# Loads and small stages of a decoder layer's input projection moved to other steps of its plan

## The chip, the cores and the metric

One core of a Trainium2 chip. The metric is the device time of one execution, in microseconds (us), as the median of several runs. The engines are TensorE (PE, with its weight loads PEld), VectorE (DVE), ScalarE (ACT), GpSimd (POOL) and SyncE (SP), which only issues DMAs. Each engine and each issuing queue takes its instructions in program order.

## The reference

One layer of a decoder on 2048 prompt rows and on 8 samples of 4 rows each, all in float32. What matters here is its beginning: an RMS norm, one input projection to five column groups, a layer norm and a gating product on one of them, and for the samples attention over a cache of 2048 keys.

```python
def _project(x, g, w_in):
    z = _rmsnorm(x, g) @ w_in
    return jnp.split(z, [D_ATT, 2 * D_ATT, 3 * D_ATT, 3 * D_ATT + D_SGU], axis=-1)
...
def _spatial_gate(vc, w_s, b_s):
    T = vc.shape[-3]
    causal = jnp.tril(jnp.ones((T, T), dtype=w_s.dtype))
    wm = w_s[:, :T, :T] * causal
    return jnp.einsum('gts,...sgc->...tgc', wm, vc) + b_s[:, :T].T[:, :, None]
...
    q, k, v, u, vg = _project(x, norm1_g, w_in)
    ...
    att = _merge_branches(outs, lses).reshape(B, S, D_ATT).astype(x.dtype)
    vn = _layernorm(vg, sgu_ln_g, sgu_ln_b)
    vn = vn.reshape(B, S // CHUNK, CHUNK, N_GROUPS_SGU, SGU_GROUP_DIM)
    gate = _spatial_gate(vn, sgu_w, sgu_b).reshape(B, S, D_SGU)
    x = x + jnp.concatenate([att, u * gate], axis=-1) @ w_out
    x = x + _swiglu(x, norm2_g, w_gate, w_up, w_down)
```

In the attention, scores get a bias by relative distance from a small table (`rel_bias`), masked where no key lies; for the samples the three dilated branches are taken in one softmax.

## The kernel before

The kernel runs three long parts one after another: the input projection, the prompt's attention, and the output projection with the feed-forward. The change is all in the first.

**The plan.** The first part is written as a plan of about 240 steps. `at(step, phase, fn)` puts a function into it; `Plan.run` sorts by step, then by phase (early, exp, low, scores, turn, mid, values, out, misc, store), then by the order of the `at` calls, and calls each. The scheduling is manual, so this is also each engine's program order. An instruction that waits holds up whatever follows it on its engine; a DMA whose buffer is not free holds up whatever follows it on its queue. Nearly all DMAs go out on SP; the sample's query loads (L530) and the four new rows of a key tile (L519) go out on ACT.

**The projection.** Two halves of 8 row tiles (128 rows each); in each half the five column groups, in the order q, k, u, g, v and then u, g, q, k, v; for each column group the row tiles in groups of 3, 3 and 2; for each of these 8 steps, one for each 128 rows of the weights (k). So a column group is 24 steps, a half is 120. A step's `products` (L318 to L320) are three matmuls for each row tile, since each operand is split into a high and a low part (xh*wh, xh*wl, xl*wh); in the first half the groups of two also take the samples' rows (L323), two matmuls. Results go to PSUM: two double banks (`ps_s`) in turn, and two single ones (`ps_o`) for the third of a group. A bank must be read out before the next group but one may write it.

**Weights.** Piece n (0 to 79) is 128 x 512, loaded by `w_load` (L215) and split into `wh` by ACT (L220) and `wl` by DVE (L226), six steps ahead of its first use. Pieces 0 to 7 are loaded at the very beginning into two wide tiles (`w_first`, four slots each). All others go through `raw` tiles, of which there are three, nine steps ahead of their use. The wide tiles serve again for the split gate rows (`vnh`, `vnl`) from step 84.

**What follows the products.** q and k are scaled by ACT (`zn`, L330), transposed on PE (L344), split (L349, L350) and stored. u is scaled (L402). g is scaled in PSUM (L334) and then goes through a layer norm: statistics on DVE (`layer_norm_a`, L366), a square root on ACT (L374), a product on DVE that frees the bank (`layer_norm_c`, L379), scale and bias on ACT and POOL (L382, L383). `gate_split` splits the result on ACT (`vnh`, L135) and POOL (`vnl`, L138). For each group of four row tiles follow four gate products on PE (`gates`, L412), their bias and product with u on DVE (`gates_u`, L420), four transposes (`gated`, L426), copies and stores. The small results on PE (`ps_t`) share two banks in turn.

**Tables and masks.** `gate_loads` (L263 to L271) and `gate_diagonal` (L274) fetch the gate's matrices, `gate_masks` masks and splits them. `table` (L482) makes the prompt's bias rows, stored by L485; `table_spread` (L488, L489) copies them from DRAM to DRAM into one shifted row per partition and head, 1024 rows of 640 and 1024 rows of 128 numbers. `sample_table` (L501) makes the samples' bias `bias_s`.

**The samples.** For each sample b and row t, `key_unit` (L536) multiplies a query with three key tiles (u = 0, 1, 2), and `key_sum` (L541) adds up over each head on DVE. The u = 0 units run on DVE, most others on POOL. For samples 0 to 2 the units u = 1, 2 run at steps 36 to 59 and u = 0 at 60 to 74; from sample 3 on, from step 76, all three run together, three units in four steps, to step 155. A key tile is loaded three steps ahead (L518, L522). Then come `sample_bias` (L557), the softmax for each half of the samples (`softmax_a`, `_e`, `_b`, `_c`: L562 to L584, with an exponential on ACT), and products with the values (L596).

The lines of the plan that are touched are the calls of `at` near L642 to L673, L723 to L729 and L759 to L766.

Of the kernel before, what the change touches and what calls it, by code (L numbers as in the profile page):

```python
# [10 lines left out]
F32 = mybir.dt.float32  # L11
# [8 lines left out]
P = 128  # L20
# [3 lines left out]
KD = D // P  # L24
H = 8
# [4 lines left out]
SB = 8  # L30
ST = 4
# [33 lines left out]
def hymba_step(ctx: ExitStack, tc: tile.TileContext, A: dict, O: dict):  # L65
# [9 lines left out]
    turn = [0, 0, 0, 0]  # L75
# [85 lines left out]
    at = plan.at  # L161
# [13 lines left out]
    def raw_tile():  # L175
        return rp.tile([P, 512], F32, name="raw", tag="raw", bufs=RAW)
# [32 lines left out]
    W = {}  # L209

    def w_load(n):
        half, ki, k = n // (5 * KD), n // KD % 5, n % KD
        c0 = COL[ORDER[half][ki]]
        W[n, "r"] = r = raw_tile()
        sync.dma_start(r, A["w_in"][k * P:(k + 1) * P, c0:c0 + 512])  # L215

    def w_high(n):
# [335 lines left out]
        unit["hm"] = sp.tile([P, DA], F32, name="hm", tag="kn", bufs=2)  # L553
        sync.dma_start(unit["hm"], A["headmask"])

    def sample_bias():
        dve.tensor_add(S, S, bias_s.broadcast_to([P, 3, SB, ST * H]))  # L557

    def softmax_a(bg):
        pt = ps_t()  # L560
# [80 lines left out]
                x_half(*first[n][1:])  # L641
    for n in range(KD, 2 * 5 * KD):  # L642
        need = n // KD * 24 + n % KD
        at(need - 9, "misc", w_load, n)
        at(need - 6, "early", w_high, n)
        at(need - 6, "mid", w_low, n)
    for t, s0, s1 in ((3, -1, 1), (4, 0, 2), (5, 2, 5), (6, 6, 10), (7, 8, 13)):
# [11 lines left out]
        at(s0, "early", norm1_scale, a, b)  # L659
    at(12, "misc", sample_load)  # L660
    at(15, "out", sample_split)
    at(42, "misc", gate_loads)
    for b in range(SB):
        at(44 + b, "misc", gate_diagonal, b)
    at(54, "out", gate_masks)
    at(56, "misc", table_loads)
    at(60, "turn", table, 0, 512, l12_d[:, 0:512])
    at(61, "turn", table, 512, 256, l12_d[:, 512:768])
    at(62, "turn", table, 768, 256, l3_d)
    at(63, "misc", sample_table_load)  # L670
    at(65, "misc", table_spread)
    at(70, "turn", sample_table)

    V0 = 168
    for s0, r in ((V0 - 1, [0]), (170, [0, 3]), (B0, [0, 1])):
# [2 lines left out]
    for half in range(2):  # L678
        for ki, kind in enumerate(ORDER[half]):
            for gi, tiles in enumerate(GROUPS):  # L680
# [13 lines left out]
                for j, tj in enumerate(tiles):  # L694
# [15 lines left out]
                    if kind in "qk":  # L710
                        which = "qk".index(kind)
                        at(e + 1, "turn", transposed, which, kind, t)
                        if kind == "k":
                            at(e + 1, "store", store_rows, kind, t)
                        at(e + 2, "early", transposed_split, which, t)
                        at(e + 2, "store", store_transposed, which, t)
                    elif kind == "v":
                        at(e + 1, "store", store_values, t)
                        at(e + 1, "store", store_rows, kind, t)
                    else:  # L720
                        layer_norm(e + 1, t, lambda t=t: zn["g", t], P, lambda t=t: gate_tile(t))

                        f = e + 4 + (3 if tj in (4, 5) else 0)  # L723
                        at(f, "turn", gate_split, t)
                        if tj % 4 == 3:
                            g = t // 4
                            for x in range(4):
                                at(f + 2 + x, "turn", gates, g, x)
                                at(f + 3 + x, "early", gates_u, g, x)  # L729
                            for x in range(4):  # L730
                                at(f + 6 + x, "turn", gated, g, x)
                                at(f + 7 + x, "early", gated_copy, g, x)
                                at(f + 7 + x, "store", store_gated, g, x)
# [13 lines left out]
    for run in key_runs:  # L747
        for j, (b, t, u) in enumerate(run):
# [7 lines left out]
            at(s0, "out", key_unit, b, t, u, pool if u == 1 or u == 2 and b >= EARLY else dve)  # L756
            at(s0 + 1, "out", key_sum, b, t, u)
            i += 1
    at(159, "early", sample_bias)  # L759
    at(159, "out", values_start)  # L760
    for bg in range(2):
        s0 = V0 - 8 + bg * 32
        at(s0, "turn", softmax_a, bg)
        at(s0 + 1, "early", softmax_e, bg)
        at(s0 + 3, "early", softmax_b, bg)
        at(s0 + 5, "turn", softmax_c, bg)  # L766
# [1314 lines left out]
```

## Time and profile before

| | |
|---|---|
| median of 3 runs | 2550.32 us (2549.67 to 2557.51) |
| profiled execution, its time | 2553.33 us |
| its span, first to last instruction | 2551.4 us |
| PE busy | 2447.2 us (96%) |
| DVE, ACT, POOL busy | 1275.1, 1129.6, 1292.2 us (50, 44, 51%) |
| mean granted TensorE clock | 0.984 |
| DMA moved | 455.37 MB, mean 178 GB/s |

How to read the profile. A row of the timeline is: start in us from the span's start, duration, engine, source line, operation, result and operands, shapes, count, and in brackets the idle time of the engine just before it with what ended it. SPq and ACTq are DMAs being issued on these queues; their duration is that of the issue, not of the transfer. A row of the windows is: the stretch, its length, the busy time of PE, weight loads, DVE, ACT and POOL with the number of instructions, the granted share of the TensorE clock, the busy share of the 16 DMA engines, and GB/s. Idle time of an engine that is not the bottleneck costs nothing by itself.

### The profile page before, as it was taken

To read this page: it belongs to the slowest core of one execution; us is meant where nothing else is said; L and a number is where in the kernel's file an instruction comes from. 1 tells how busy PE (TensorE), PEld (TensorE's weight loads), DVE (VectorE), ACT (ScalarE), POOL (GpSimd) and SP (SyncE) were. 2 spreads that over 40 slices of the span, in tenths; PEclk is the share of its full clock that TensorE was granted. 3 is DMA by queue.
4 is the path that set the end of the run, shared out by engine and by line. 5 is a ranking of instruction groups with operands and counts; after the bars stand their busy time and mean duration, and the time that the engine had idled before them with its cause. 6 is when DMAs were issued, how large, how long until landed. Compare 5 with 4: busy or idle time off the path is not lost.

```text
span 2551.4 us, 39141 instructions
## 1 busy us (share of the span) xinstructions
PE 2447.2 (96%) x14022; PEld 2120.1 (83%) x14022; DVE 1275.1 (50%) x2598; ACT 1129.6 (44%) x2438; POOL 1292.2 (51%) x1012
## 2 busy tenths in 40 slices
PE   8999999999999898999999999999999998999997
PEld 6777786667888678899899988999999986999996
DVE  4448674216777644443444465444444465444445
ACT  6414333226666556545445355332323345444432
POOL 2116442004777636667677543553645534666662
PEclk9999999999999899999999999999999998999998
DMA  8964735675554463536546471563544543665552
GB/s 260 281 220 150 255 115 164 200 252 197 174 178 151 116 205 112 182 128 198 169 143 201 139 220 62 203 214 128 204 163 160 203 152 122 224 206 192 197 193 106
DMA packets 292149, 455.37 MB, mean 178 GB/s; under 512 B 28695, under 2 KB 160968, under 8 KB 286836
## 3 DMA queue, kind: packets, MB, share of 16 engines
q1 hardware_dynamic: 285108, 440.82, 52.7%
q10 hardware_dynamic: 6848, 12.06, 1.6%
q8 instruction: 111, 1.82, 0.3%
q14 instruction: 82, 0.67, 0.1%
HBM read 365.07 MB, written 157.84 MB: 205 GB/s over the span
## 4 chain that ended last, share of the span: by engine, by line
PE 55%; POOL 9%; issue 7%; ACT 4%; DVE 4%; DMA 2%; SPq 0%; POOLq 0%; ACTq 0%; DVEq 0%
PE ps_o L1647 13%; PE ps_m L1576 8%; PE ps_m L1575 8%; PE ps_m L1574 8%; POOL op L1517 3%; PE ps_s L853 2%; PE ps_o L908 2%; DMA ab_d<-pair 2%; ACT fr L1485 1%; PE ps_t L880 1%; PE ps_s L932 1%; POOL pair L1497 1%; POOL pair L1506 1%; POOL fr L1500 1%; POOL dw L138 1%
## 5 line engine op out<-in xcount | busy, mean ns | idle before, releaser
L1517 POOL TENSOR_TENSOR op<-fr,op 128x512 fp32r<-128x512 f32 x385 | 488.3, 1297 | 313.2 <-ACT op L1513 291.6
L1574 PE MATMUL ps_m<-xh,op 128*128 128x384 f32 (+3 forms) x1904 | 605.2, 318 | 0.0
L1575 PE MATMUL ps_m<-xl,op 128*128 128x384 f32 (+3 forms) x1904 | 604.2, 317 | 0.9 <-POOL xl L138 0.9
L1576 PE MATMUL ps_m<-xh,op 128*128 128x384 f32 (+3 forms) x1904 | 604.6, 318 | 0.0
L1647 PE MATMUL ps_o<-dw,hw 128*128 128x512 f32 x2040 | 484.0, 392 | 15.7 <-DVE acc L1649 14.4
L1647 PEld LDWEIGHTS ps_o<-dw,hw 128*128 128x128 f32 x2040 | 379.5, 188 | 98.6 <-DVE acc L1649 20.7
L1575 PEld LDWEIGHTS ps_m<-xl,op 128*128 128x128 f32 x1904 | 360.3, 189 | 4.8 <-POOL xl L138 1.1
L1574 PEld LDWEIGHTS ps_m<-xh,op 128*128 128x128 f32 x1904 | 360.7, 189 | 4.0
L1576 PEld LDWEIGHTS ps_m<-xh,op 128*128 128x128 f32 x1904 | 360.1, 189 | 0.1
L1649 DVE TENSOR_TENSOR acc<-acc,ps_o 128x512 f32<-128x512 f32 (+1 forms) x362 | 247.1, 686 | 214.8 <-PE ps_o L1647 214.8
L1614 ACT ACTIVATE ps_t<-zn 128x384 f32<-128x384 f32 (+1 forms) x126 | 58.3, 463 | 462.1 <-DVE zn L1597 361.9
L1513 ACT ACTIVATE op<-fr 128x512 fp32r<-128x512 f32 x396 | 235.7, 623 | 24.4 <-DMA fr<-ab_d 19.7
L138 POOL TENSOR_TENSOR dw<-fd,dw 128x1024 fp32r<-128x1024 f32 x66 | 158.5, 2402 | 121.7 <-ACT dw L135 121.7
L318 PE MATMUL ps_s<-wh,xh 128*128 128x512 f32 x480 | 199.7, 416 | 10.6 <-ACT xh L135 6.0
L319 PE MATMUL ps_s<-wl,xh 128*128 128x512 f32 x480 | 191.7, 399 | 1.8 <-DVE wl L226 1.8
L320 PE MATMUL ps_s<-wh,xl 128*128 128x512 f32 x480 | 191.3, 399 | 0.0
L1517 POOL TENSOR_TENSOR op<-pair,op 128x512 fp32r<-128x512 f32 x63 | 81.4, 1301 | 116.4 <-ACT op L1513 116.4
L318 PEld LDWEIGHTS ps_s<-wh,xh 128*128 128x128 f32 x480 | 92.5, 193 | 54.2 <-issue 23.7
L536 POOL TENSOR_TENSOR pr<-kv,qb 96x512 f32<-96x512 f32 x32 | 47.2, 1479 | 178.1 <-DMA qb<-zs_d 61.6
L1624 ACT ACTIVATE hw<-ps_t 128x384 fp32r<-128x384 f32 (+1 forms) x126 | 56.1, 453 | 175.1 <-DVE ps_t L1620 174.1
L924 POOL CAST sq<-k 128x512 fp32r<-128x512 f32 x32 | 34.0, 1062 | 164.3 <-PE ps_s L319 164.3
L320 PEld LDWEIGHTS ps_s<-wh,xl 128*128 128x128 f32 x480 | 92.3, 192 | 20.6 <-DVE xl L138 0.3
(456 smaller groups left out, 4296.6 us busy)
## 6 DMA issues: line engine op xcount, KB each, us to landing
fr<-ab_d SPq DMA_DIRECT2D x308, 256.0 KB
fd<-in_w_down_dram SPq DMA_DIRECT2D x66, 512.0 KB
out_ks_dram<-in_cache_k_dram SPq DMA_DIRECT2D x56, 512.0 KB
out_vs_dram<-in_cache_v_dram SPq DMA_DIRECT2D x56, 512.0 KB
ab_d<-fr SPq DMA_DIRECT2D x88, 256.0 KB
raw<-in_w_in_dram SPq DMA_DIRECT2D x72, 256.0 KB
qk_d<-pair SPq DMA_DIRECT2D x64, 256.0 KB
ab_d<-pair SPq DMA_DIRECT2D x63, 256.0 KB
```

Of the source, the lines that this page charges most:

```text
L138: (eng_lo or pool).tensor_sub(lo, src, hi.bitcast(F32))
L318: pe.matmul(o[j], xh[:, k, :], wh, start=(k == 0), stop=False)
L319: pe.matmul(o[j], xh[:, k, :], wl, start=False, stop=False)
L320: pe.matmul(o[j], xl[:, k, :], wh, start=False, stop=(k == KD - 1))
L1513: act.activation(ops[f, j][0], ab[f][j], AF.Copy)
L1517: (pool if f or j in POOL_LOW else dve).tensor_sub(lo_, ab[f][j], hi.bitcast(F32))
L1574: pe.matmul(out, wh[:, ks], xh[:, :, k], start=(k == 0), stop=False)
L1575: pe.matmul(out, wh[:, ks], xl[:, :, k], start=False, stop=False)
L1576: pe.matmul(out, wl[:, ks], xh[:, :, k], start=False, stop=(k == 3))
L1614: act.activation(g, c, AF.Silu)
L1647: pe.matmul(ps[0:nr], l_, r_[:, cs], start=(z == 0 and y == 0), stop=(z == FC - 1 and y == len(pairs) - 1))
L1649: dve.tensor_add(B.acc[i][0:nr, cs], B.acc[i][0:nr, cs], ps[0:nr])
```

## The change

- Weight pieces 8 to 31 (the other column groups k, u, g of the first half) are loaded into the eight slots of the first wide tiles and not into `raw`, and earlier: pieces 8 to 15 at steps 6 to 20 (before: 15 to 22), 16 to 23 at steps 19 to 40 (39 to 46), 24 to 31 at steps 43 to 64 (63 to 70). The splits stay where they are.
- `gate_loads`, `gate_diagonal` and `gate_masks` go five steps later; `table_loads` from 56 to 62, `table` from 60-62 to 70-72, `sample_table_load` from 63 to 73, `table_spread` from 65 to 75, `sample_table` from 70 to 82.
- In the first half the gate products of both groups of four go two steps later (first group 94 to 96, second 104 to 106), with all that follows them; the split of tiles 4 and 5 goes two steps later too.
- `sample_bias` is done for each half of the samples, at steps 134 and 159 (before: once, at 159), and the first half's softmax runs at steps 136 to 141 (before 160 to 165). The second half's stays at 192.

```diff
-        W[n, "r"] = r = raw_tile()
+        W[n, "r"] = r = w_first[k // 4][:, k % 4].bitcast(F32) if n < 4 * KD else raw_tile()
...
-    def sample_bias():
-        dve.tensor_add(S, S, bias_s.broadcast_to([P, 3, SB, ST * H]))
+    def sample_bias(bg):
+        s = S[:, :, bg * 4:bg * 4 + 4]
+        dve.tensor_add(s, s, bias_s.broadcast_to([P, 3, 4, ST * H]))
...
-        at(need - 9, "misc", w_load, n)
+        at(max(need - 29 + 2 * (n % KD), 6 + 2 * (n % KD)) if n < 4 * KD else need - 9, "misc", w_load, n)
...
-    at(42, "misc", gate_loads)
+    at(47, "misc", gate_loads)
     for b in range(SB):
-        at(44 + b, "misc", gate_diagonal, b)
-    at(54, "out", gate_masks)
-    at(56, "misc", table_loads)
-    at(60, "turn", table, 0, 512, l12_d[:, 0:512])
-    at(61, "turn", table, 512, 256, l12_d[:, 512:768])
-    at(62, "turn", table, 768, 256, l3_d)
-    at(63, "misc", sample_table_load)
-    at(65, "misc", table_spread)
-    at(70, "turn", sample_table)
+        at(49 + b, "misc", gate_diagonal, b)
+    at(59, "out", gate_masks)
+    at(62, "misc", table_loads)
+    at(70, "turn", table, 0, 512, l12_d[:, 0:512])
+    at(71, "turn", table, 512, 256, l12_d[:, 512:768])
+    at(72, "turn", table, 768, 256, l3_d)
+    at(73, "misc", sample_table_load)
+    at(75, "misc", table_spread)
+    at(82, "turn", sample_table)
...
-                        f = e + 4 + (3 if tj in (4, 5) else 0)
+                        f = e + 4 + ((3 if half else 5) if tj in (4, 5) else 0)
                         at(f, "turn", gate_split, t)
                         if tj % 4 == 3:
                             g = t // 4
+                            f += (2, 2, 0, 0)[g]
                             for x in range(4):
                                 at(f + 2 + x, "turn", gates, g, x)
...
-    at(159, "early", sample_bias)
+    at(134, "early", sample_bias, 0)
+    at(159, "early", sample_bias, 1)
...
-        s0 = V0 - 8 + bg * 32
+        s0 = (136, V0 + 24)[bg]
```

## The prediction, made before the changed kernel was run

> **What bounds the kernel now.** I read the page first, then the TensorE rows that begin with idle time, then busy time by windows, then the queues around each wait. TensorE (PE) is busy 96% of the span, so the time is the work of PE plus what PE waits.
>
> ```profile
> PE 2447.2 (96%) x14022; PEld 2120.1 (83%) x14022; DVE 1275.1 (50%) x2598; ACT 1129.6 (44%) x2438; POOL 1292.2 (51%) x1012
> ...
> PEclk9999999999999899999999999999999998999998
> ```
>
> The edits all lie in the first part, the input projection of 240 steps, which ends near 582 us; what follows is untouched and starts when PE gets there, so time won or lost on PE in this part is taken as won or lost at the end. The PE rows with idle time before them (in brackets, with what ended it):
>
> ```profile
> 119.54 1.12 PE L344 MATMUL ps_t<-ident,zn 128*128 128x128 f32 x4 [4.79 <-ACT zn L330]
> ...
> 183.16 0.79 PE L318 MATMUL ps_s<-wh,xh 128*128 128x512 f32 x1 [3.55 <-ACT wh L220]
> ...
> 214.93 0.44 PE L323 MATMUL ps_o<-wh,xs 128*64 128x512 f32 x1 [0.86 <-DVE zn L379]
> ...
> 226.35 0.38 PE L412 MATMUL ps_t<-vnh,wg_h 128*128 128x256 f32 x1 [1.48 <-ACT vnh L135]
> ...
> 235.60 0.38 PE L412 MATMUL ps_t<-vnh,wg_h 128*128 128x256 f32 x1 [2.66 <-DVE un L420]
> ...
> 310.31 0.50 PE L319 MATMUL ps_s<-wl,xh 128*128 128x512 f32 x1 [1.80 <-DVE wl L226]
> ...
> 382.05 0.55 PE L582 MATMUL ps_t<-ident,S_s 128*128 128x128 f32 x3 [1.03 <-DVE S_s L576]
> 384.76 0.38 PE L412 MATMUL ps_t<-vnh,wg_h 128*128 128x256 f32 x1 [0.80 <-ACT vnh L135]
> ...
> 391.79 0.39 PE L412 MATMUL ps_t<-vnh,wg_h 128*128 128x256 f32 x1 [2.09 <-DVE un L420]
> ```
>
> The projection's 2000 matmuls come in the order of the plan, so counting them gives each step its time. Below: window, its length, busy time of PE, weight loads, DVE, ACT, POOL, granted clock, DMA share and GB/s. The first window is two undisturbed steps of nine matmuls: 4.08 us, so 2.04 a step and 0.227 a matmul.
>
> ```profile
> 192.14:196.22 4.08, 4.08 (x19) 3.38 (x18) 3.88 (x7) 1.44 (x4) 0.00 (x0) 1.00 0.90 287
> ...
> 254.94:266.01 11.07, 11.07 (x62) 9.59 (x60) 6.92 (x16) 3.50 (x5) 6.51 (x5) 1.00 0.77 240
> 164.89:169.57 4.68, 4.68 (x34) 3.96 (x32) 0.75 (x1) 1.25 (x2) 0.00 (x0) 1.00 0.52 195
> ...
> 110.73:124.08 13.35, 8.55 (x31) 6.64 (x30) 9.25 (x19) 5.10 (x9) 3.97 (x2) 0.74 0.94 287
> 175.37:190.10 14.73, 11.18 (x37) 8.40 (x36) 6.26 (x11) 3.27 (x5) 0.00 (x0) 0.77 0.81 255
> 212.54:215.44 2.90, 2.04 (x9) 1.32 (x8) 2.76 (x9) 1.30 (x3) 2.90 (x4) 1.00 0.54 148
> 222.86:240.76 17.90, 12.80 (x59) 9.74 (x58) 17.48 (x40) 9.13 (x16) 8.26 (x6) 0.90 0.57 173
> 308.12:315.89 7.77, 5.96 (x20) 4.44 (x18) 7.19 (x9) 0.72 (x2) 5.96 (x4) 0.78 0.86 273
> 379.50:394.70 15.20, 10.32 (x46) 7.59 (x45) 14.13 (x34) 8.91 (x16) 5.51 (x4) 0.89 0.55 173
> ```
>
> From them: steps 103 to 106 carry four gate products, (11.07 - 4 x 2.04) / 4 = 0.73 each. Step 69 carries the sample bias product, 4.68 - 8 x 0.227 = 2.87. Six places lose time, with the natural time of their steps taken off:
> A, steps 47 to 49: 13.35 - 6.4 (26 matmuls 5.9, a group of transposes with its tail 0.5) = 7.0.
> B, steps 73 to 76: 14.73 - 8.16 = 6.6.
> C, step 88: 2.90 - 1.81 = 1.1.
> D, steps 93 to 96, with four gate products: 17.90 - 10.4 = 7.5.
> E, steps 127 and 128: 7.77 - 4.08 = 3.7.
> F, steps 164 to 167, with three gate products: 15.20 - 7.8 = 7.4.
> Sum 33.3 us, the most that can be had here. Part of each is the clock: in E the idle time is 1.80, the other 1.89 is PE at a granted mean of 0.78. I charge 1.9 for a wait of 1.8 to 4 us, nothing for one below 1 us (C: granted 1.00).
>
> [...]
>
> **The change part by part.** *Weights, A.* ACT splits the third set of weights at steps 42 to 49; there it sat 8.28 us for a load into three raw buffers, behind nine gate loads on the one SP queue:
>
> ```profile
> 101.51 0.42 SPq L263 DMA_DIRECT2D xr<-in_sgu_wT_dram  x1
> ...
> 109.41 0.34 SPq L215 DMA_DIRECT2D raw<-in_w_in_dram  x1
> ...
> 114.29 0.72 ACT L220 ACTIVATE wh<-raw,g1c 128x512 fp32r<-128x512 f32 x1 [8.28 <-DMA raw<-in_w_in_dram]
> ```
>
> Now these 24 loads go to the eight slots of the first weights: weights 8 to 15 at steps 6 to 20, 16 to 23 at 19 to 40, 24 to 31 at 43 to 64, nine steps or more ahead of the split, and a slot is free a step before its load. The gate loads also go five steps later. A is gone; what is late next is the sample keys' loads, which share a full DMA stretch (0.94 in A's window); no PE product hangs on them before step 56. I take -6.5, ends -7.0 and -4. The same loads now run among the first x tiles: each is 0.42 us of SP and 256 KB, 0.9 us at the 287 GB/s of A's window, ahead of x tile 6. ACT turned that tile just before the first scaling:
>
> ```profile
> 30.64 0.67 ACT L330 ACTIVATE zn<-ps_s,rstdn 128x512 f32<-128x512 f32 x1
> ...
> 33.52 0.60 PE L344 MATMUL ps_t<-ident,zn 128*128 128x128 f32 x4
> ```
>
> Between its end, 31.31, and its transposes are 2.2 us, so that is covered: +0.4, ends 0 and +2.
>
> *Bias tables, B, C and D.* The spread of the tables (two DMAs, L488 and L489) held SP, and what was behind it:
>
> ```profile
> 157.64 0.39 PE L318 MATMUL ps_s<-wh,xh 128*128 128x512 f32 x1
> ...
> 158.69 0.71 SPq L488 DMA_DIRECT2D b_d<-l_d  x1
> 159.45 8.54 SPq L489 DMA_DIRECT2D b_d<-l_d  x1
> 168.08 9.55 SPq L518 DMA_DIRECT2D kv<-in_cache_k_dram  x1
> ...
> 181.69 0.69 DVE L536 TENSOR_TENSOR pr<-kv,qb 100x512 f32<-100x512 f32 x1 [15.34 <-DMA kv<-in_cache_k_dram]
> ...
> 182.38 0.72 ACT L220 ACTIVATE wh<-raw,g1c 128x512 fp32r<-128x512 f32 x1 [16.24 <-DVE pr L536]
> ```
>
> A key load behind it reached DVE 23.0 us after the spread's issue; DVE stood 15.34, ACT with it, and PE ran out of weights (B). With the weights long loaded and the spread at step 75, B is gone: -6.6 (end -5). But the same hold now lies over steps 75 to 87, and there the gate's layer norms begin. The load behind it (b 3, t 1, step 77) feeds DVE's key product at step 80, which stands in DVE's order ahead of the norm of tile 0 at step 81. PE needs the three norms' banks at step 88. They took, from the first statistic to the third product's end (214.13 + 0.74 = 214.87), 11.5 us:
>
> ```profile
> 203.34 0.69 DVE L366 BATCH_NORM_STATS2 bn<-ps_s 128x6 f32<-128x512 f32 x1
> ...
> 214.13 0.74 DVE L379 SCALAR_TENSOR_TENSOR zn<-ps_o,mv,lng 128x512 f32<-128x512 f32 x1
> ```
>
> Count from the start of step 75. The spread goes out about 1 us in, as it did against step 65, which began at 157.64. The key load lands between 20.5 (the queue's 0.71 + 8.54 + 9.55 and a landing) and 23.0 later; I take 21.5, since in the runs of three units one query load serves three key products, not one, and less shares the engines. Key product 0.65, norms 11.5: the third bank is free at 34.7. PE comes to it after 13 x 2.04 + 2.87 (sample bias product, now at step 82) + six matmuls 1.36 = 30.8. So PE waits 3.9 where it waited 0.86, and with the clock C costs 5.8 instead of 1.1.
>
> From there DVE leads. In the trace the sixth norm ended 18.4 us after the third, and the first gate's result came after it:
>
> ```profile
> 232.56 0.74 DVE L379 SCALAR_TENSOR_TENSOR zn<-ps_o,mv,lng 128x512 f32<-128x512 f32 x1
> ...
> 234.68 0.86 DVE L420 SCALAR_TENSOR_TENSOR un<-ps_t,sgb,un 128x256 f32<-128x256 f32 x2
> ```
>
> The first gate products go from steps 94-97 to 96-99, so `vnh` and `vnl` are there in time (226.35's wait goes). But step 96 itself needs the sixth norm's bank: from 215.44, seven steps of 1.81, one gate product and 1.36 bring PE there at 230.2, and the bank is free at 233.3: 3.1 of waiting. The third product at step 98 needs the first one's L420, now behind two more weight lows, a key product and sums, about 5.2 after the sixth norm: 1.7; the fourth 0.6. With the clock 7.3, against 7.5. C and D together: +4.5, ends 0 (key load landing sooner, less DVE work in between) and +8. I take +3.2, nearer to the low end, because DVE's rows there hold operations drawn out by POOL that need not fall the same way. The second group's products go two steps later behind a DVE that is level by then: nothing. Tables, their PE products and gate masks only move: nothing.
>
> *First softmax, F.* At steps 160 to 165 it put two table loads into ACT amid the norms:
>
> ```profile
> 375.04 1.28 ACT L571 ACT_TABLE_LOAD   x1 [1.11 <-DVE nm L566]
> 376.34 0.58 ACT L571 ACTIVATE S_s<-ps_t,nm 128x384 f32<-128x384 f32 x1
> ...
> 377.64 1.28 ACT L374 ACT_TABLE_LOAD   x1
> ...
> 330.17:341.05 10.88, 10.88 (x50) 9.01 (x48) 9.09 (x11) 5.71 (x9) 3.77 (x3) 1.00 0.62 191
> ```
>
> That kept the norm of tile 11 some 3 us, then the products at 384.76 and 391.79. At steps 136 to 141 there are no norms. Steps there take 10.88 / 8 = 1.36; five are 6.8 us. The chain between is transposes and maximum, 1.0; table load 1.28; exponential 0.58 and its sum 0.2; then in program order a weight split on ACT and one on DVE, a key sum and the scaling, 0.7 each (like L379): 5.9 in all, covered by 0.9. The weights split next are due at step 144. +0.5, ends 0 and +2.5. At 166 to 168, with the norms' own pace, a wait near 1.5 remains: -5.7, ends -7.4 and -2. The bias add is one operation made two halves; DVE has room for the extra issue, and the second half leaves step 159 shorter.
>
> [...] The row's next ACTIVATE starts 0.02 after the load, so the row's price stands.
>
> *E.*
>
> ```profile
> 304.87 5.38 DVE L226 SCALAR_TENSOR_TENSOR wl<-raw,g1c,wh 128x512 fp32r<-128x512 f32 x1 [1.89 <-ACT wh L220]
> ```
>
> E's cause, a DVE weight split drawn out to 5.38 us while POOL works (5.96 us of E's window), is not edited; it may fall otherwise: 0, ends -3.7 and +2.
>
> Sum: -6.5 + 0.4 - 6.6 + 3.2 + 0.5 - 5.7 = -14.7. The profiled execution took 2553.33 (span 2551.4), 3.0 above the median 2550.32; on the median 2535.6, say 2535 with a little of E.
>
> **The rivals.** *All covered*: the key load lands near 20.5 and DVE is quick, C and D cost what they did, F goes whole, E does not recur: -7.0 - 6.6 - 7.4 - 3.7 = -24.7, 2526. For it: DVE is busy only half the span. Against: the program order of the key product ahead of the norm.
> *Traded*: the hold lands in full, C and D +8, A only -4, F only -2, B -5: with the small terms -2, 2548. For it: 15.34 us of standing DVE now among norms.
> *Slower*: DVE never catches up after step 87, and each of the eight first-half gate products waits 2.66 as at 235.60: 21.3 and four clock dips 7.6 against D's 7.5 give +21.4, C +4.7; with the other terms -17.9 it is +8.2, 2558.5. It decides where each product's L420 ends some 2.7 us after PE has reached the product two after it, in both groups. Against: in 254.94:266.01 four products pass with PE busy throughout.
>
> **How the numbers follow.** Forecast 0.63 (2528 to 2543), all covered 0.20, traded 0.12, slower 0.05. Two runs of this kernel can be told apart from about 0.3%, 7.7 us: faster means below 2542.7: 0.63 + 0.20 and a little of traded, 0.85; same 0.10; slower 0.05. The range leaves out half of traded, slower and the far end of the covered case: 2524 to 2545.
>
> **What would show it.** No ACT idle on `raw` at steps 42 to 49 and no PE wait at L344 and `wh`; a DVE wait on `kv` of 10 us or more behind the spread, just ahead of the first L366; PE waits at step 88 on `zn` L379 of 2 to 5 us; one at the first matmul into `ps_o` of step 96; the first ACT_TABLE_LOAD pair split, one at step 137, one at the first norm of the second half. Wrong would be: no DVE wait ahead of L366 (too slow a forecast), or new PE waits before step 42 or at the L562 and L582 transposes (too fast).

## The result, and the profile after

The changed kernel took 2535.05 us in the median of 5 runs (2529.02 to 2536.74), the kernel before 2550.32 in 5 (2547.61 to 2557.51): ratio 0.9931, 95% interval 0.9910 to 0.9951. That is 15.3 us less; 14.7 was worked out for the sum and 2535 forecast. One execution of the changed kernel in experiment 5 (3241.91 us, granted clock 0.693) and one of the kernel before that was taken along with experiments 5 to 8 (4855.10 us) stand far off all others and are left out of medians and ratios. The profiled execution of the changed kernel took 2529.02, 6 under its median, with a span of 2526.9. The engines' row of the page after:

```profile
PE 2436.6 (96%) x14022; PEld 2112.4 (84%) x14022; DVE 1268.6 (50%) x2599; ACT 1130.4 (45%) x2438; POOL 1290.7 (51%) x1012
```

PE is still the bound. Its busy time is 10.6 us shorter than before with the same 14022 matmuls: fewer of them ran at half clock (mean granted clock 0.989, before 0.984). That is less than half of what the span lost; the rest is idle time. Within the projection PE's busy time is 6.5 us shorter and its idle time 10.4.

The PE rows with idle time before them, kernel after, in the first part. The last is the third matmul of the attention; the projection ends just ahead of the first:

```profile
202.62 0.44 PE L323 MATMUL ps_o<-wh,xs 128*64 128x512 f32 x1 [1.77 <-DVE zn L379]
...
221.08 0.80 PE L318 MATMUL ps_o<-wh,xh 128*128 128x512 f32 x1 [3.00 <-DVE zn L379]
...
226.91 0.39 PE L412 MATMUL ps_t<-vnh,wg_h 128*128 128x256 f32 x1 [0.82 <-DVE un L420]
...
230.43 0.38 PE L412 MATMUL ps_t<-vnh,wg_h 128*128 128x256 f32 x1 [0.48 <-DVE un L420]
...
369.31 0.38 PE L412 MATMUL ps_t<-vnl,wg_h 128*128 128x256 f32 x1 [1.32 <-POOL vnl L138]
...
373.15 0.38 PE L412 MATMUL ps_t<-vnh,wg_h 128*128 128x256 f32 x1 [1.62 <-DVE un L420]
...
449.04 1.01 PE L344 MATMUL ps_o<-ident,zn 128*128 128x128 f32 x4 [2.04 <-ACT S_s L572]
...
566.20 0.38 PE L856 MATMUL ps_s<-k,qh 128*128 128x256 f32 x1 [0.39 <-DVE st L862]
```

Before, that last row began at 583.06:

```profile
583.06 0.39 PE L853 MATMUL ps_s<-k,qh 128*128 128x256 f32 x1 [0.39 <-DVE st L859]
```

So 16.9 us were won in the projection. The span is 24.5 shorter; the other 7.6 lie behind 566 us, in work that the change does not touch. From its end to the end of the span the twelve traces of this study differ between 1959 and 1970 us, so those 7.6 belong to the two executions, and it is the projection's 16.9 that answers to the forecast's 14.7.

Windows of the kernel after (length; busy time of PE, weight loads, DVE, ACT, POOL; granted clock; DMA share; GB/s): steps 47 to 49 (A), 73 to 76 (B), 81 to 83, 88 (C), 95 to 98 (D), 127 and 128 (E), 164 to 168 (F), 192 and 193:

```profile
109.47:115.85 6.38, 6.38 (x31) 5.17 (x30) 6.38 (x11) 3.18 (x6) 1.30 (x1) 1.00 0.96 267
164.13:172.29 8.16, 8.16 (x37) 6.76 (x36) 6.64 (x11) 1.98 (x3) 0.00 (x0) 1.00 0.80 233
180.45:191.16 10.71, 10.71 (x52) 8.87 (x51) 0.90 (x2) 0.00 (x0) 0.40 (x1) 0.84 0.61 213
199.32:203.13 3.81, 2.04 (x9) 1.32 (x8) 3.63 (x11) 1.24 (x3) 3.81 (x4) 1.00 0.36 115
214.01:231.25 17.24, 12.95 (x61) 10.19 (x59) 16.51 (x38) 6.46 (x12) 10.41 (x7) 0.90 0.50 158
294.59:300.67 6.08, 4.60 (x19) 3.22 (x18) 3.46 (x5) 1.05 (x2) 5.38 (x3) 1.00 0.98 317
364.67:378.84 14.17, 11.17 (x58) 8.89 (x57) 13.22 (x32) 7.75 (x14) 6.19 (x4) 1.00 0.65 206
444.66:454.29 9.63, 7.59 (x31) 5.04 (x30) 2.75 (x5) 5.52 (x9) 0.00 (x0) 0.82 0.43 132
```

A and B run at their natural length with PE busy throughout. The third row has PE busy throughout too, but at a granted 0.84; the last at 0.82: two losses that the forecast did not have.

The hold of the spread, on SP's queue and on DVE:

```profile
169.73 0.71 SPq L488 DMA_DIRECT2D b_d<-l_d  x1
171.00 5.33 SPq L489 DMA_DIRECT2D b_d<-l_d  x1
176.44 9.71 SPq L518 DMA_DIRECT2D kv<-in_cache_k_dram  x1
```

```profile
190.26 0.69 DVE L536 TENSOR_TENSOR pr<-kv,qb 100x512 f32<-100x512 f32 x1 [13.89 <-DMA kv<-in_cache_k_dram]
190.87 0.69 DVE L366 BATCH_NORM_STATS2 bn<-ps_s 128x6 f32<-128x512 f32 x1
...
201.82 0.74 DVE L379 SCALAR_TENSOR_TENSOR zn<-ps_o,mv,lng 128x512 f32<-128x512 f32 x1
...
220.28 0.74 DVE L379 SCALAR_TENSOR_TENSOR zn<-ps_o,mv,lng 128x512 f32<-128x512 f32 x1
```

The key load reaches DVE 20.5 us after the spread's issue; DVE stands 13.89 us, directly ahead of the first layer norm; the third norm ends at 202.56 and the sixth at 221.02, 18.5 later. That is the chain the forecast wrote down.

### The profile page after: what moved, and what is told of

The parts are those of the page before. It is cut to its first block, busy times and chain, and to the rows that moved or that the text cites. A ratio compares the mean times of both kernels' runs of the same rounds, so it can differ in the third digit from the quotient of the medians.

```text
span 2526.9 us, 39131 instructions
## 1 busy us (share of the span) xinstructions
PE 2436.6 (96%) x14022; PEld 2112.4 (84%) x14022; DVE 1268.6 (50%) x2599; ACT 1130.4 (45%) x2438; POOL 1290.7 (51%) x1012
## 4 chain that ended last, share of the span: by engine, by line
PE 56%; POOL 8%; issue 7%; DMA 4%; DVE 3%; ACT 3%; SPq 1%; POOLq 0%; ACTq 0%; DVEq 0%
PE ps_o L1650 13%; PE ps_m L1579 8%; PE ps_m L1578 8%; PE ps_m L1577 8%; PE ps_s L856 2%; POOL op L1520 2%; PE ps_o L911 2%; DMA ab_d<-pair 2%; PE ps_t L883 1%; ACT fr L1488 1%; PE ps_s L935 1%; POOL pair L1500 1%; PE ps_s L318 1%; POOL fr L1503 1%; POOL dw L138 1%
## 5 line engine op out<-in xcount | busy, mean ns | idle before, releaser
L1650 PE MATMUL ps_o<-dw,hw 128*128 128x512 f32 x2040 | 484.0, 392 | 15.7 <-DVE acc L1652 14.4
L1650 PEld LDWEIGHTS ps_o<-dw,hw 128*128 128x128 f32 x2040 | 379.5, 188 | 98.6 <-DVE acc L1652 20.7
L1627 ACT ACTIVATE hw<-ps_t 128x384 fp32r<-128x384 f32 (+1 forms) x126 | 56.2, 454 | 175.0 <-DVE ps_t L1623 174.0
```

What stands on the lines that cost most here:

```text
L1650: pe.matmul(ps[0:nr], l_, r_[:, cs], start=(z == 0 and y == 0), stop=(z == FC - 1 and y == len(pairs) - 1))
```

## The experiments

Lengths of places, by counting the 2000 matmuls as in the prediction. "Natural" is the length without a wait at full clock, in the changed kernel's order (77 to 87 hold the sample bias product there, 22.4 without it; before, 93 to 99 are 18.0 and 164 to 168 are 10.6). The last row is the start of the attention's row shown above, less its 0.39 of idle time. Ratios are to the kernel before, taken along with each experiment. The intervals of most versions overlap, so what tells them apart are the stretches of one trace each, and the two traces of the changed kernel end 2.6 us apart.

| us | natural | before | after | after, again | weights only | tables back | softmax back | spread at 121 | pieces | pieces, keys on POOL | pieces, exp. 8 | gates back | last version |
|---|---|---|---|---|---|---|---|---|---|---|---|---|---|
| 47-49 | 6.4 | 13.4 | 6.4 | 6.4 | 6.4 | 6.4 | 6.4 | 6.4 | 6.4 | 6.4 | 6.4 | 6.4 | 6.4 |
| 50-72 | 48.3 | 51.3 | 48.3 | 48.3 | 56.2 | 57.2 | 48.3 | 48.3 | 48.3 | 48.3 | 48.3 | 48.3 | 48.3 |
| 73-76 | 8.2 | 14.7 | 8.2 | 8.2 | 8.9 | 8.2 | 8.2 | 8.2 | 8.2 | 8.2 | 8.2 | 8.2 | 8.2 |
| 77-87 | 25.3 | 22.4 | 27.0 | 28.6 | 22.4 | 22.4 | 25.8 | 25.4 | 27.0 | 25.4 | 27.1 | 27.1 | 26.1 |
| 88 | 1.8 | 2.9 | 3.8 | 1.8 | 1.8 | 1.8 | 5.0 | 1.8 | 1.8 | 1.8 | 1.8 | 4.0 | 1.8 |
| 93-99 | 17.0 | 25.4 | 23.3 | 22.7 | 24.1 | 22.7 | 23.3 | 20.8 | 20.6 | 22.2 | 20.0 | 23.8 | 21.4 |
| 122-134 | 26.5 | 30.2 | 28.6 | 28.7 | 28.5 | 27.0 | 28.0 | 43.2 | 31.4 | 30.7 | 32.7 | 30.4 | 28.2 |
| 164-168 | 10.4 | 18.0 | 14.2 | 14.2 | 19.5 | 14.4 | 20.7 | 14.2 | 14.5 | 16.3 | 14.8 | 14.2 | 14.5 |
| 192-193 | 5.8 | 7.6 | 9.6 | 7.6 | 7.4 | 7.5 | 7.9 | 7.3 | 7.5 | 6.7 | 5.8 | 6.9 | 5.8 |
| end |  | 582.7 | 565.8 | 563.2 | 570.4 | 564.9 | 571.4 | 573.0 | 562.6 | 563.2 | 569.3 | 568.5 | 557.9 |

Where tables or sample product lie in 50 to 72 (before, weights only, tables back), its natural length is 51.3; the kernels with the gate products two steps earlier have 18.0 in 93 to 99; in experiment 8 one of them and the first transposes that follow lie behind step 99.

**1. The weights alone**, in the kernel before:

```diff
-        W[n, "r"] = r = raw_tile()
+        W[n, "r"] = r = w_first[k // 4][:, k % 4].bitcast(F32) if n < 4 * KD else raw_tile()
-        at(need - 9, "misc", w_load, n)
+        at(max(need - 29 + 2 * (n % KD), 6 + 2 * (n % KD)) if n < 4 * KD else need - 9, "misc", w_load, n)
```

> The kernel before with the weights part alone (the 24 loads into the first weights' slots, at the new steps). Theory (each place pays for itself): A goes whole, so steps 47 to 49 take 6.4 us instead of 13.35 and no ACT wait on raw is seen at steps 42 to 49. B: ACT no longer needs the slots that DVE frees late, but DVE still stands some 15 us on the key load behind the spread and the weight lows of steps 76 on stand behind it, so B loses 3 to 5 us instead of 6.6. C to G as before. The projection ends 9 to 11 us earlier than 583.06; time ratio about 0.996. Rival 1 (B's whole cause is the late weight load): B goes too, and the projection ends 13 to 14 us earlier. Rival 2 (the early loads only move the queue's jam): x tiles or key loads come late elsewhere before step 73, and less than 5 us is left.

Measured: 2542.47 us, ratio 0.9967 (0.9954 to 0.9980); the projection ends 12.3 earlier. A is gone whole. Of B 0.7 is left at 73 to 76, but 4.9 came ahead of it, nearly all at step 72, so the spread at step 65 still costs 5.6 instead of 6.6. The size was as in the theory, the path was not. ACT rows, then a PE row, of this run:

```profile
168.50 0.28 ACTq L519 DMA_DIRECT2D kv<-zs_d  x1
168.83 0.72 ACT L220 ACTIVATE wh<-w,g1c 128x512 fp32r<-128x512 f32 x1 [15.01 <-DMA b_d<-l_d]
```

```profile
170.18 0.79 PE L318 MATMUL ps_o<-wh,xh 128*128 128x512 f32 x1 [3.59 <-ACT un L402]
```

ACT, which issues the small rest of a key tile itself (L519, its issue at 168.50), stood 15.01 until the spread landed, and behind it a scaled u. Even with the weights already there, ACT had to wait. L519 reads nothing that the spread writes. In this trace and in experiment 2's its issue waits for semaphore 102, which the spread's first DMA (L488) signals when it lands, so the wait comes from a shared semaphore and not from data. The way through DVE's key product, which the prediction read in the kernel before, is only one of those by which the spread reached PE.

**2. The tables back at their old steps**, in the changed kernel (gate loads 42, diagonals 44, masks 54, table loads 56, tables 60 to 62, sample table 63, spread 65, sample product 70).

> The changed kernel with the gate and bias tables (loads, products, spread, sample table) back at the old steps; weights, gate products and softmax as changed. Theory (the spread's hold costs wherever DVE has work behind it): the hold lies again over steps 65 to 76; B costs 3 to 5 us by late weight lows; in exchange C falls from 2.0 lost to about 1, D from 6.4 to 0 to 2, and the clock dip of 1.6 at steps 81 to 83 may go with the sample product's place. Sum between -6 and -1 against the changed kernel: the move of the tables by itself was no gain. Rival (the move of the tables is what took B away): B costs 6.6 again and D stays near 6, so the kernel is 5 to 7 us slower than the changed one.

Measured: 2538.20 us, ratio 0.9951 (0.9935 to 0.9968). The interval overlaps with the changed kernel's, and its projection ends 0.9 earlier than the first profile of that and 1.7 later than the second: the tables' move by itself won nothing that can be seen. The theory's gain of 1 to 6 was not reached. Of the 5.9 us lost at steps 50 to 72, 1.6 are a wait at the table products, whose loads were now late, 3.4 are half clock after the sample product (row below), and only 0.9 a wait behind the spread: what PE had lost ahead of that wait was taken off it.

```profile
158.22:172.99 14.77, 13.91 (x58) 10.71 (x57) 0.75 (x1) 1.30 (x2) 0.00 (x0) 0.77 0.59 215
```

D, which the theory had falling to 0 to 2, stayed at 5.7. So the spread's hold is not all of D.

**3. The softmax back at step 160** (and the bias add in one operation at 159):

```diff
-    at(134, "early", sample_bias, 0)
-    at(159, "early", sample_bias, 1)
+    at(159, "early", sample_bias)
-        s0 = (136, V0 + 24)[bg]
+        s0 = V0 - 8 + bg * 32
```

> The changed kernel with the first softmax and the one bias add back at steps 159 to 165. Theory (table loads amid the norms): steps 164 to 167 lose 7.4 us again instead of 3.7, with two table loads of 1.28 at the norms, and everything before step 136 stays; the projection ends 3 to 4.5 us later than the changed kernel's. Rival (F's rest is set by the norms' own pace and the first wait is only renamed): less than 1.5 us difference.

Measured: 2535.59 us, ratio 0.9951 (0.9934 to 0.9969); the projection ends 5.6 (first profile) to 8.3 (second) later. Window of steps 164 to 168, and its longest PE wait:

```profile
363.53:384.26 20.73, 14.51 (x59) 11.37 (x58) 16.40 (x41) 10.20 (x19) 5.30 (x4) 0.84 0.46 142
```

```profile
376.70 0.58 PE L412 MATMUL ps_t<-vnh,wg_h 128*128 128x256 f32 x1 [3.44 <-DVE un L420]
```

F came back, and larger: 20.7 against 18.0 before, with the same waits in the same order but 3.44 where 2.09 stood. With the old place it took 18.0, 19.5 and 20.7 in three programs, with the new one 14.2 to 14.5 in seven traces, 14.8 in experiment 8 and 16.3 in experiment 7, where half clock followed the wait for `un`. By these stretches the first softmax's place is worth 4 to 6.5 us; the intervals of the whole times overlap.

**4. The spread at step 121**

```diff
-    at(75, "misc", table_spread)
+    at(121, "misc", table_spread)
```

> The changed kernel with only the two spread DMAs moved from step 75 to step 121, where neither norms nor weight lows stand behind a key product. Theory (the spread's hold of SP, through the key load and DVE, is what C and D lose): no DVE wait of 10 us ahead of the first L366; the PE wait at step 88 (1.77) and the one into ps_o at step 96 (3.00) go, with the 0.82 and 0.48 behind them; C and D together lose 0 to 2 us instead of 8.4; the hold now stands at steps 122 to 133 and costs 0 to 2 there. The projection ends 6 to 8.5 us earlier than the changed kernel's. Rival 1 (DVE is too slow at the norms by itself, as C's 1.1 and D's 7.5 before the change could say): C and D keep 4 us or more. Rival 2 (the hold is as dear at steps 121 to 133, by late x tiles 14 and 15): 4 us or more lost there.

Measured: 2541.85 us, ratio 0.9966 (0.9955 to 0.9977), the projection ending 7.1 later than the changed kernel's: rival 2. C went whole and D fell from 6.3 to 3.8, as in the theory. But PE stood at step 128, and DVE ahead of it:

```profile
306.76 0.76 PE L318 MATMUL ps_o<-wh,xh 128*128 128x512 f32 x1 [12.49 <-DVE zn L445]
```

```profile
305.88 0.74 DVE L445 SCALAR_TENSOR_TENSOR zn<-ps_o,rstds,zn 32x512 f32<-32x512 f32 x1 [13.35 <-DMA out_vp_dram<-zn]
```

Rival 2 had the size, but not the way, which was not late x tiles. The one thing behind the spread that was overlooked: the sample rows' result on DVE frees a bank of the third group, and DVE stood 13.35 first, until a store issued behind the spread (L358) had landed. At step 75 and at step 121 alike the one long transfer was dear by the work behind it on the queue: DVE stood 13.89 us and 13.35.

**5. The changed kernel once more**

> The changed kernel itself, a second profiled execution of the same program. It tells which of the small differences belong to the program and which to the execution. Theory (waits are set by the order written out, so they repeat; half-clock stretches begin on a fixed grid of about 3.41 us and follow a stretch of the grid in which PE stood or ran tiny matmuls for some 1.8 us or more, so they need not repeat): the waits at steps 88, 96, 97, 98, 165, 166 come again within 0.5 us of 1.77, 3.00, 0.82, 0.48, 1.32, 1.62; the half clock after the sample bias product (1.6 us lost at steps 81 to 83) and the one after step 192's wait may come or go, and where the first goes, the wait at step 88 grows by what it no longer covers. Projection's end within 2 us of 565.64. Rival (half clock follows from the amount of idle time before it alone): both half-clock stretches come again.

Measured: 2534.70 us in the median of five, ratio 0.9934 (0.9910 to 0.9959), the projection ending 2.6 earlier than in the first profile. The waits at 165 and 166 came again as 1.34 and 1.59. Here 3.3 us went at steps 81 to 83 in two stretches of half clock instead of 1.7 in one; PE then came to step 88 so late that nothing was left to wait for (1.81), and step 96 waited 2.40 instead of 3.00. Step 97 missed the theory's bound: 2.11 instead of 0.82. The 2.04 at step 192 came as 1.57, and no half clock followed. Of the two half-clock stretches one came back and one did not, against the rival.

**6. The spread in eight pieces**

```diff
-    def table_spread():
-        sync.dma_start(b_d[:, :, 0:640], dap(l12_d, 127, [[768, H], [-1, P], [1, 640]]))
-        sync.dma_start(b_d[:, :, 640:768], dap(l3_d, 127, [[256, H], [-1, P], [1, P]]))
+    def table_spread(j):
+        p = 16 * j
+        sync.dma_start(b_d[:, p:p + 16, 0:640], dap(l12_d, 127 - p, [[768, H], [-1, 16], [1, 640]]))
+        sync.dma_start(b_d[:, p:p + 16, 640:768], dap(l3_d, 127 - p, [[256, H], [-1, 16], [1, P]]))
-    at(75, "misc", table_spread)
+    for j in range(8):
+        at(75 + 3 * j, "misc", table_spread, j)
```

> The changed kernel with the spread cut into eight pieces of 16 rows each (two DMAs a piece, same bytes), one piece every third step from 75 to 96. Theory (the cost of the spread is that one long transfer stands ahead of key loads on one queue; cut, each load waits at most some 2.4 us more, which the three steps of lead cover): no DVE wait of 10 us ahead of the first L366, no PE wait at step 88; at steps 93 to 99 what the run with the spread at 121 showed, 3 to 5 us lost instead of 6.3, since there DVE's own 18.5 us from third to sixth norm is the rate; nothing lost at steps 122 to 134 beyond 2. Projection ends 3 to 6 us earlier than the changed kernel's. Rival (the spread's bytes themselves crowd the transfers, however they are cut): key loads late again by 5 us or more in all, and C and D keep 7 us or more.

Measured: 2529.43 us, ratio 0.9911 (0.9890 to 0.9932). A piece on SP, and the first layer norm on DVE:

```profile
167.45 0.72 SPq L489 DMA_DIRECT2D b_d<-l_d  x1
168.22 0.63 SPq L490 DMA_DIRECT2D b_d<-l_d  x1
170.32 0.33 SPq L519 DMA_DIRECT2D kv<-in_cache_k_dram  x1
```

```profile
178.32 0.70 DVE L366 BATCH_NORM_STATS2 bn<-ps_s 128x6 f32<-128x512 f32 x1 [2.54 <-ACT ps_s L334]
...
194.46 0.74 DVE L379 SCALAR_TENSOR_TENSOR zn<-ps_o,mv,lng 128x512 f32<-128x512 f32 x1
...
214.01 0.74 DVE L379 SCALAR_TENSOR_TENSOR zn<-ps_o,mv,lng 128x512 f32<-128x512 f32 x1
```

The hold is gone: the first norm waits only for its own input, the wait at step 88 is gone, D loses 3.6. So it is not the bytes as such: the same bytes, cut and spaced by three steps, hold up nothing. Whether cutting alone would do, with all pieces at step 75, was not run. The end is 3.3 earlier than in the first profile of the changed kernel, the low end of the forecast, and only 0.6 earlier than in the second: 4.9 went at steps 122 to 134 (2 in the changed kernel), where PE waited 2.54 for the low half of an x tile on DVE.

**7. Pieces, and four key products given from DVE to POOL**

```diff
-pool if u == 1 or u == 2 and b >= EARLY else dve)
+pool if u == 1 or u == 2 and b >= EARLY or u == 0 and 84 <= s0 <= 96 else dve)
```

> The kernel with the spread in pieces, and besides the four key products of the first kind at steps 84 to 96 given from DVE to POOL. Theory (D's rest is DVE's rate between third and sixth norm): the time from third to sixth norm's end falls from 18.5 to 15.5 to 17.5, and steps 93 to 99 lose 0 to 2.5 us. Rival 1 (POOL holds up DVE more than it relieves it): the time from third to sixth norm stays at 18 us or grows, with DVE operations beside POOL drawn out over 1 us. Rival 2 (POOL becomes late with the low halves of the norms): a PE wait on vnl takes the place, steps 93 to 99 lose 3 us or more.

Measured: 2530.19 us, ratio 0.9915 (0.9893 to 0.9936); steps 93 to 99 took 22.2, losing 5.2 where 0 to 2.5 were expected, and the projection ends 0.7 later than with the pieces alone. Between third and sixth norm DVE has fewer products, but waits for POOL's:

```profile
194.71 0.74 DVE L379 SCALAR_TENSOR_TENSOR zn<-ps_o,mv,lng 128x512 f32<-128x512 f32 x1
...
198.29 0.69 DVE L542 TENSOR_REDUCE S_s<-pr 128x8 f32<-128x512 f32 x1 [1.82 <-POOL pr L537]
200.75 0.70 DVE L366 BATCH_NORM_STATS2 bn<-ps_s 128x6 f32<-128x512 f32 x1 [1.78 <-ACT ps_s L334]
...
215.21 0.74 DVE L379 SCALAR_TENSOR_TENSOR zn<-ps_o,mv,lng 128x512 f32<-128x512 f32 x1
```

20.5 from third to sixth norm, against 18.5 in the changed kernel and 19.6 with the pieces alone. The theory that the products on DVE set this rate fell; the nearest is rival 1, but by key sums that wait for POOL, not by DVE operations drawn out.

**8. Pieces, and gate products and second softmax at other steps**: the first group's products at 98 to 101, the third's at 166 to 169, the second softmax at 190 to 195.

> The kernel with the spread in pieces, and besides the first group's gate products two steps later again (98 to 101), the third group's one step later (166 to 169), and the second softmax two steps earlier (190 to 195). Theory (each remaining wait is a matter of a few us of lead): steps 93 to 103 lose 0 to 2 us, steps 164 to 168 lose 0 to 2 instead of 3.7, step 192 waits under 0.5 us instead of 1.3 to 2.0 and no half clock follows there. Projection ends 8 to 13 us earlier than the changed kernel's, time ratio to the kernel before 0.988 to 0.991. Rival (the third group's products are held by the banks, of which there is one from step 167 to 169, and by DVE's rate): steps 164 to 171 lose as much as before, only later, and less than 6 us is won in all.

Measured: 2534.82 us, ratio 0.9927 (0.9904 to 0.9950), the projection ending 6.8 later than with the pieces alone. Only the softmax did what was expected: steps 192 and 193 took 5.8, their natural length. The gate products did not: steps 93 to 121 took 77.1, with the pieces alone 71.3, and the waits went along with them:

```profile
226.88 0.58 PE L412 MATMUL ps_t<-vnh,wg_h 128*128 128x256 f32 x1 [3.17 <-DVE un L420]
...
236.85 0.47 PE L426 MATMUL ps_t<-ident,un 128*128 128x128 f32 x1 [2.80 <-DVE un L420]
...
379.35 0.38 PE L412 MATMUL ps_t<-vnh,wg_h 128*128 128x256 f32 x1 [2.73 <-DVE un L420]
```

`un` (L420) is issued on DVE a step after its product, among other DVE work that comes first in the order; a later product only finds another neighbour ahead of its L420.

**9. The gate products back at steps 94 and 104**, in the changed kernel:

```diff
-                        f = e + 4 + ((3 if half else 5) if tj in (4, 5) else 0)
+                        f = e + 4 + (3 if tj in (4, 5) else 0)
-                            f += (2, 2, 0, 0)[g]
```

> The changed kernel with the first two groups' gate products back two steps earlier, at steps 94 to 97 and 104 to 107, all else as changed. Theory (DVE leads from the first norm on and PE meets the same DVE results wherever the products stand): a wait on vnh or vnl comes at step 93, one on un two products later; steps 93 to 103, which lost 6.2 us with the products two steps later, lose 7 to 10; the second group is as level as before, nothing lost at 104 to 113. Projection ends 1 to 4 us later than the changed kernel's 563.0 to 565.6. Rival (the two steps of lead are what lets the products pass at all): more than 4 us lost besides; or, the other way, the wait only changes its name and the end does not move by 1 us.

Measured: 2533.87 us, ratio 0.9928 (0.9908 to 0.9947). The waits have the old names again, POOL's low half and `un`:

```profile
216.73 0.38 PE L412 MATMUL ps_t<-vnl,wg_h 128*128 128x256 f32 x1 [0.96 <-POOL vnl L138]
...
224.65 0.39 PE L412 MATMUL ps_t<-vnh,wg_h 128*128 128x256 f32 x1 [2.68 <-DVE un L420]
```

Steps 93 to 121, over which the products and their transposes move, took 73.5 us, in the changed kernel 74.0 and 73.4: the wait changes its name, as the second rival had it for these steps. The end is nevertheless 2.7 to 5.3 later, by other places: half clock after step 88's wait (1.6 at step 89) and 1.7 at steps 122 to 134. The move of the gate products won nothing.

**10. The last version**: pieces, the second softmax at 190 to 195, the 24 sample matmuls in three lots, x tile 13's split one step earlier:

```diff
-    at(82, "turn", sample_table)
+    for a in range(3):
+        at(81 + a, "turn", sample_table, a)
-        s0 = (136, V0 + 24)[bg]
+        s0 = (136, V0 + 22)[bg]
-        at(s0 + 2, "out", x_split, 8 + j, dve if j % 2 else pool)
+        at(s0 + (1 if j == 5 else 2), "out", x_split, 8 + j, dve if j % 2 else pool)
```

> The kernel with the spread in pieces, and besides the second softmax two steps earlier (190 to 195), the sample bias product's 24 tiny matmuls spread over steps 81 to 83, eight in each, and the split of x tile 13 one step earlier, ahead of the sample rows on DVE. Theory (each takes away a wait that the runs showed, or the stretch of tiny matmuls that counts as idle): no half clock at steps 81 to 87, which take 25.3 to 25.5 us for 77 to 87 however the grid falls; no wait above 0.5 at step 192 and no half clock there; steps 122 to 134 lose 0 to 2 us instead of 5. Projection ends at 553 to 559 us, 4 to 10 earlier than with the pieces alone, time ratio to the kernel before 0.986 to 0.990. Rival (the order on DVE and POOL near step 125 only shuffles the wait): 122 to 134 lose 3 us or more, and the end is less than 4 us earlier.

Measured: 2525.74 us in the median (2523.20 to 2529.50), ratio to the kernel before 0.9900 (0.9880 to 0.9919). The projection ends 4.6 earlier than with the pieces alone, 5.2 to 7.9 earlier than in the changed kernel. Windows of steps 80 to 83, and 127 and 128:

```profile
179.08:190.88 11.80, 11.80 (x62) 9.42 (x60) 5.94 (x18) 2.51 (x7) 3.79 (x3) 1.00 0.61 197
290.32:296.05 5.73, 4.68 (x20) 3.23 (x19) 5.73 (x7) 0.74 (x2) 3.91 (x3) 1.00 0.95 291
```

No half clock, though three lots cost 0.7 us more than one (26.1 for steps 77 to 87, above the 25.5 expected); 1.7 lost at 122 to 134; nothing at 192. What remains is D with 4.4 and F with 4.1. The parts of this version were not run one by one, so how much of the 122 to 134 is due to x tile 13's split is not shown.

## Why the prediction was right

The sum was -14.7 against the profiled execution; the projection gave -16.9 in the first profile after, -19.5 in the second. That the sum came so near is in part luck, since misses cancelled: in the first profile F fell short by 1.9 and step 192 cost 2.1, while C and D, E and the start gave 1.8, 1.7 and 1.1 more than the sum had. The forecast's steps, by first profile and second:

- **A**, -6.5: measured -7.0 in both, and alone in experiment 1. No ACT idle on `raw`, no PE wait at L344. A slip in the reading: seven gate loads, not nine, stand ahead of the load that ACT waited for.
- **Early loads**, +0.4: steps 8 to 23 took 0.2 and 1.6 longer, within the 0 to +2; steps 0 to 7 were shorter by more, so no cost of these loads is seen.
- **B**, -6.6: measured -6.6. The way from the spread to PE was incomplete: experiment 1 shows ACT held by the spread's own landing, 15.01 us, with the weights long loaded. It did no harm, because the spread moved too.
- **C and D**, +3.2 taken, +4.5 worked out: measured +1.4 and +0.5, with the half clock at steps 81 to 83 counted in. Point by point: the key load landed 20.5 after the spread's issue (21.5 taken, 20.5 the lower bound); the third bank was free 34.4 after the start of step 75 (34.7); the wait at step 96 was 3.00 and 2.40 (3.1), at the third gate product 0.82 and 2.11 (1.7), at the fourth 0.48 and 0.49 (0.6). What failed is PE's arrival at step 88: 32.6 after the start of step 75 instead of 30.8, because after the sample product PE ran at half clock, which was not in the sum. So it waited 1.77 there and not 3.9, or not at all: what PE had lost ahead of this wait was not lost twice.
- **E**, 0: measured -1.7 and -1.5, within the ends. The change did not cure it: nine of the twelve traces have this weight low drawn out to 5.29 to 5.44 us (before, 5.38), the second profile among them, and PE waits 0.6 to 3.1 us for it. In the second profile the wait was 1.35 instead of 1.80 and no half clock followed; in the first the weight low was not drawn out. Steps 122 to 134 lose 0.5 to 6 us in the programs without the spread there. Why was not settled, so this part of the gain is luck. The row of the second profile:

```profile
290.36 5.29 DVE L226 SCALAR_TENSOR_TENSOR wl<-raw,g1c,wh 128x512 fp32r<-128x512 f32 x1 [1.88 <-ACT wh L220]
```

- **Softmax's new place**, +0.5: no wait at steps 136 to 143. The 0.7 more that steps 135 to 143 take are the transposes that came with it. The load of the table, 1.28, stood where nothing waited for ACT; the next came at the second half's first norm:

```profile
316.33 1.28 ACT L572 ACT_TABLE_LOAD   x1 [1.14 <-DVE nm L567]
...
343.17 1.28 ACT L374 ACT_TABLE_LOAD   x1
```

- **F**, -5.7: measured -3.8 in both, transposes counted in. This is the term that was mis-sized. The forecast left one wait near 1.5; there were two, 1.32 for POOL's `vnl` and 1.62 for `un`, and with what goes with them 3.8 us of the 7.4 stayed. The `vnl` wait stood in the trace before too (0.97, behind the 0.80 on `vnh`), and I read both as the softmax's doing:

```profile
386.11 0.39 PE L412 MATMUL ps_t<-vnl,wg_h 128*128 128x256 f32 x1 [0.97 <-POOL vnl L138]
```

- **Not in the sum**: the start, -1.1 and -2.3 over steps 0 to 7 (19.1 to 21.4 in the twelve traces, with no pattern by program); step 24's rest of a wait, -0.3; step 192, +2.1 and 0.0. There the wait grew from 1.55 to 2.04 in one profile, and half clock followed; in the other it was 1.57, and none followed.

Of the rivals, "all covered" came near at C, and "traded" at F; "slower" is out: DVE stays level from the second group on, in all runs with the hold at step 75.

What the experiments change in the reading: the gain is that of the weights (7.0) and the softmax (4 to 6.5). Getting the spread off the weights' path took away B, but the new place brought back 4.3 and 3.3 us at steps 77 to 99 by its hold and by half clock, measured against the tables at their old steps. The moves of the tables as a whole and of the gate products by themselves won nothing measurable (experiments 2 and 9). That the spread's hold costs C and part of D is shown (4 and 6); what sets the rest of D, 18.5 us from third to sixth norm with DVE busy 16.0 of them, is not only the key products (7), and stays open beyond that.

## What to carry to other kernels

Look at what one long DMA has behind it, on its own queue and on every engine that issues or waits in order: moving it only moved the hold here (13.35 us on DVE with the spread at step 121, 13.89 at 75), and cutting it into eight pieces three steps apart took the hold away (the first norm waited 2.54 us, for its own input). A product moved later to escape a wait gained nothing where the producer's engine was the one that led (steps 93 to 121 took 73.5 us with the gate products back, 74.0 and 73.4 with them moved); compare whole stretches, since the wait only changes its name. Price a wait on PE with the clock in mind: in these traces up to 1.74 us of waiting within one of the 3.41 us stretches described below cost itself, 1.92 or more there some 1.7 us besides (half of the 3.41 that then ran at half clock), and time lost ahead of a wait was taken off it (at step 88 a wait of 1.77 where 3.9 was worked out).

## What the runs showed of the hardware

**Where half clock began.** In each trace all stretches of half clock begin on one grid of about 3.413 us, whose place differs from execution to execution (in the projection of the kernel after at 186.39, 220.51 and 449.20, apart by 10 and 67 such steps). I took the grid's stretches of the projection, from PE's first matmul on, from all twelve traces, those that ran at full clock and held none of the sample product's matmuls. Each of the 24 in which PE stood 1.92 us or more was followed by one at half clock, and none of the more than 1800 with 1.74 or less; of the four between, 1.76 and 1.81 were, 1.78 and 1.90 were not. In the kernel after, for one, PE stood 2.43 us from 217.09 to 220.51, and the next stretch was at 0.50; it stood 1.78 from 200.03 to 203.44, and the next was at 1.00. The prediction's E, 1.80 us idle, lies between. The traces show when half clock came; they do not show what brings it about.

**Half clock after the sample product.** The sample product is 24 matmuls of 8 columns each, 2.84 us, with PE busy throughout. In some traces half clock follows it, in others not, and this went with how the product fell into the grid. The time of those matmuls alone in two neighbouring stretches of the grid, and in a second fence the stretch after them with all instructions, kernel after:

```profile
179.55:182.97 3.42, 0.38 (x4) 0.39 (x4) 1.00 0.52 207
182.97:186.39 3.42, 2.46 (x23) 2.37 (x22) 1.00 0.53 192
```

```profile
186.39:189.80 3.41, 3.41 (x9) 2.63 (x8) 0.00 (x0) 0.00 (x0) 0.00 (x0) 0.50 0.92 293
```

The same in experiment 7, where the product falls across the border:

```profile
180.45:183.86 3.41, 1.21 (x11) 1.21 (x11) 1.00 0.38 127
183.86:187.27 3.41, 1.64 (x15) 1.54 (x14) 1.00 0.00 0
```

```profile
187.27:190.69 3.42, 3.42 (x17) 2.83 (x16) 3.11 (x10) 2.19 (x5) 1.29 (x1) 1.00 0.22 77
```

2.46 of it in one stretch, and the next is at 0.50; 1.64, and the next is at 1.00. In the eleven traces with the product in one lot, six have 2.13 or more in one stretch, and half clock follows in all six; five have 1.88 or less, and it follows in none.
